# Four features computed singly at the entry of the channel mix, instead of two singly and two started early, with the block sums, splits and weight pieces there in another order

## The chip, the cores and the metric

One NeuronCore of a Trainium2 chip runs one program. The metric is the device time of one execution in microseconds; the time of a kernel is the median of its runs. Engines are named as in the profile: PE is TensorE (PEld its weight loads), ACT is ScalarE, DVE is VectorE, POOL is GpSimd, SP issues DMAs.

## What is computed

One layer of a decoder for 512 prompt rows and 64 sample rows (576 in all), width 1024: a combined projection, a short convolution, three groups of dilated attention, a gated merge, and then the part that matters here:

```python
x1 = layer_norm(ALPHA * x + mixed @ w_o, ln1_g, ln1_b)
hid = jnp.square(jax.nn.relu(x1 @ w_up))                       # 1024 -> 4096
x2 = layer_norm(ALPHA * x1 + hid @ w_down, ln2_g, ln2_b)       # 4096 -> 1024
```

## The kernel before

All matrix products are in float32 precision by splitting: an operand is held as a high half (`hi`, a cast to float32r made by ACT) and a low half (`lo` = operand minus hi, made by DVE), and a product takes three matmul passes (hi·hi, hi·lo, lo·hi). Instructions are issued in the order in which the code calls them; each engine works through its own instructions in that order and waits for semaphores. No scheduler reorders them.

Weights stand in HBM as `wall`, a list of units of 128 x 1024 floats. Units 54 to 61 are `w_o`, from `FIRST_F` = 62 on come the channel mix's: four rounds (q = 0 to 3) of eight units of `w_up` (one per feature block of 128 features) and eight of `w_down`. `Stream` loads them by SP's queue into raw tiles and splits them into `hl` tiles.

`x1` is made row tile by row tile (t = 0 to 4, the last with 64 rows): output projection, layer norm, then `turn(t)`: PE transposes the tile into the bank `x1t`, ACT and DVE write it to `yT` with gain and bias, ACT casts the high half and DVE subtracts the low half into `x1hl`. `turn(4)` comes only when the last rows are done, so the products that need just the first 256 columns of `x1hl` are put ahead of it and around it.

A feature block can be computed in two ways. *Singly* (`first_half`, `second_half`): 24 matmuls over the 256 columns `FB[0]`, 24 over the other 320, then `up_post` (ACT: relu, square, cast; DVE: low half) into `hid`. Or *as a pair* of two blocks by seven products in the place of eight (Winograd's form of Strassen's scheme, `up_pair`): the activations are split in 2 x 2 blocks (rows of the contraction by 288 columns), and four block sums of them (`x_sum(m)`: `xs` by DVE, `x1T` hi by ACT and lo by DVE) meet weight pieces `hu` (the unit itself), `hs`, `hc` (sums of weight blocks), `hd` (half a unit). The weight sums come about in `raws`: two plain DMAs by SP, then an accumulating DMA by POOL, then two additions by DVE. Products go to PSUM banks `a`, `Y`, `X`; DVE combines them in `cc`, and a second product may go into `Y` only when DVE has read the first.

`Stream.queue` takes a list of items (pairs, then units of `w_down`) and lays out weight pieces: `load()` issues what the rings of buffers allow, `hi()` casts the next piece on ACT, `lo()` does the next job on DVE (a low half or an addition). The calls to these among the products set the order on ACT and DVE.

In the kernel before, `ALONE` = 2 features (62, 63) are computed singly, and `EARLY` = (2, 4): of pairs (64, 65) and (66, 67) the two product groups `a` (24 matmuls: the first feature, the first 288 columns) are computed ahead by `up_early`, from units 64 and 66 that are loaded and split with the singles. Three pairs stand in round 0. The sequence between is written out by hand (lines 1317 to 1347).

## Time and profile before

| | |
|---|---|
| median of 3 runs | 877.98 us (877.21 to 878.64) |
| the profiled execution | 878.82 us, span 876.7 us |
| granted clock of TensorE, mean | 0.98 |
| busy: PE, DVE, ACT, POOL | 837.8, 458.3, 319.0, 79.9 us |
| HBM | 128 GB/s over the span |

The span is what the profiler saw from the first to the last instruction; the 2.12 us between it and the time of the execution lie around it. Times in the profile count from the start of the span. Below, a row of a timeline gives the start, the time from its first start to its last end, engine, line, operation, tiles, count, and in brackets the idle time before and what ended it.

### The profile page before, as it was taken

The numbers are of one execution on the slowest core, as the hardware profiler recorded it, in microseconds if no ns is written. First come the engines' busy times: TensorE is split into PE (matmuls) and PEld (weight loads), VectorE is DVE, ScalarE is ACT, GpSimd is POOL, SyncE is SP. The second block draws the span as 40 slices with busy tenths as digits, with TensorE's granted clock in tenths as the row PEclk, the third lists the DMA queues.
The fourth block names the chain that finished last, engine by engine and source line by source line (L and its number), as shares of the span: only waits on it lengthen the run. The fifth ranks groups of instructions, "written<-read, shape, count | busy, mean of one in ns | idle before, by whom it ended". The sixth has DMA issues, their size and how long they took to land.

```text
span 876.7 us, 14968 instructions
## 1 busy us (share of the span) xinstructions
PE 837.8 (96%) x6300; PEld 807.8 (92%) x6300; DVE 458.3 (52%) x755; ACT 319.0 (36%) x531; POOL 79.9 (9%) x118
## 2 busy tenths in 40 slices
PE   7999999999999999999986599999999999999994
PEld 7989989999899999988875599999999999999994
DVE  6455455465324333345655663467444754466566
ACT  6111128721222222232564461156322651256331
POOL 0221000064000000010010001000100000000013
PEclk9999999999999999999997699999999999999998
DMA  9686654851112222326061446342724254353102
GB/s 351 219 303 204 210 202 138 319 195 45 43 67 90 81 81 81 96 73 227 1 168 32 124 144 146 84 133 73 214 76 118 74 193 96 86 155 100 71 32 78
DMA packets 38610, 114.51 MB, mean 131 GB/s; under 512 B 4720, under 2 KB 5040, under 8 KB 38384
## 3 DMA queue, kind: packets, MB, share of 16 engines
q1 hardware_dynamic: 34416, 103.61, 35.8%
q0 software_dynamic: 4128, 9.96, 5.9%
q8 instruction: 49, 0.80, 0.4%
q14 instruction: 17, 0.14, 0.0%
HBM read 95.69 MB, written 16.42 MB: 128 GB/s over the span
## 4 chain that ended last, share of the span: by engine, by line
PE 90%; DVE 5%; ACT 3%; issue 1%; DMA 0%; POOL 0%; DVEq 0%; ACTq 0%
PE d L1128 18%; PE zg L518 12%; PE Y L1158 8%; PE d L1121 6%; PE a L1158 6%; PE o L1034 6%; PE X L1158 5%; PE v L885 5%; PE zA L518 5%; PE zm L518 4%; PE zB L518 4%; PE zh L518 3%; PE zc L518 2%; PE zb L518 2%; PE ya L726 1%
## 5 line engine op out<-in xcount | busy, mean ns | idle before, releaser
L1128 PE MATMUL d<-hid,hu 128*128 128x288 f32 x1152 | 154.1, 296 | 0.0
L1128 PEld LDWEIGHTS d<-hid,hu 128*128 128x128 f32 x1152 | 153.8, 189 | 0.0
L269 DVE TENSOR_TENSOR hl<-raw,hl 128x1024 fp32r<-128x1024 f32 (+1 forms) x64 | 76.3, 1203 | 102.3 <-ACT hl L268 102.0
L518 PE MATMUL zg<-xhl,hl 128*128 128x288 f32 x768 | 103.7, 296 | 0.0
L518 PEld LDWEIGHTS zg<-xhl,hl 128*128 128x128 f32 x768 | 102.8, 189 | 0.0
L268 ACT CAST hl<-raw 128x1024 fp32r<-128x1024 f32 (+1 forms) x64 | 65.0, 1020 | 67.3 <-PE zA L518 28.1
L355 ACT CAST hu<-raw 128x1024 fp32r<-128x1024 f32 x45 | 46.5, 1049 | 53.1 <-PE d L1128 27.0
L378 DVE TENSOR_TENSOR hu<-raw,hu 128x1024 fp32r<-128x1024 f32 x45 | 54.3, 1217 | 1.2 <-ACT hu L355 1.2
L1121 PE MATMUL d<-hid,hu 128*128 128x320 f32 (+1 forms) x384 | 53.4, 298 | 0.0
L1121 PEld LDWEIGHTS d<-hid,hu 128*128 128x128 f32 x384 | 51.5, 189 | 0.0
L518 PE MATMUL zA<-xhl,hl 128*128 128x288 f32 x288 | 42.8, 303 | 4.6 <-ACT xhl L496 4.5
L1158 PE MATMUL a<-x1hl,hu 128*128 128x288 f32 x312 | 46.4, 297 | 0.0
L1034 PE MATMUL o<-hl,mxhl 128*128 128x512 f32 x192 | 45.6, 394 | 0.8 <-DVE m L979 0.8
L330 POOL DMA_DIRECT2D raws<-in_wall x15 | 18.1, 1207 | 306.6 <-DMA raws<-in_wall 139.0
L518 PEld LDWEIGHTS zA<-xhl,hl 128*128 128x128 f32 x288 | 40.1, 193 | 5.7 <-ACT xhl L496 4.5
L1034 PEld LDWEIGHTS o<-hl,mxhl 128*128 128x128 f32 x192 | 35.8, 188 | 9.0 <-DVE m L979 1.1
L1158 PEld LDWEIGHTS a<-x1hl,hu 128*128 128x128 f32 x312 | 43.3, 188 | 0.4
L1376 DVE TENSOR_TENSOR yT<-yT,d 128x288 f32<-128x288 f32 x32 | 13.1, 451 | 51.7 <-PE d L1128 51.7
L1158 PE MATMUL Y<-x1T,hs 128*128 128x288 f32 x180 | 28.0, 307 | 11.0 <-DVE cc L1205 11.0
L885 PE MATMUL v<-hl,xhl 128*128 128x256 f32 x288 | 37.7, 287 | 0.0
L885 PEld LDWEIGHTS v<-hl,xhl 128*128 128x128 f32 x288 | 35.3, 191 | 2.1 <-issue 1.6
L1158 PEld LDWEIGHTS Y<-x1T,hs 128*128 128x128 f32 x180 | 26.0, 197 | 11.5 <-issue 10.7
(209 smaller groups left out, 1327.5 us busy)
## 6 DMA issues: line engine op xcount, KB each, us to landing
raw<-in_wall SPq DMA_DIRECT2D x103, 512.0 KB, 4.7
raws<-in_wall SPq DMA_DIRECT2D x30, 256.0 KB, 3.8
raws<-in_wall POOLq DMA_DIRECT2D x15, 512.0 KB, 8.4
kc<-in_kc SPq DMA_DIRECT2D x8, 512.0 KB, 4.2
out_kc_out<-kc SPq DMA_DIRECT2D x8, 512.0 KB, 6.2
vc<-in_vc SPq DMA_DIRECT2D x8, 512.0 KB, 5.4
out_vc_out<-vc SPq DMA_DIRECT2D x8, 512.0 KB, 8.2
rawl<-in_wall SPq DMA_DIRECT2D x15, 256.0 KB, 3.9
```

The lines of the kernel that those rows point to most:

```text
L268: self.nc.scalar.copy(hl[:, 0, :w], raw[:, :w])
L269: self.nc.vector.tensor_tensor(hl[:, 1, :w], raw[:, :w], hl[:, 0, :w].bitcast(F32), ALU.subtract)
L330: self.nc.gpsimd.dma_start(sums, two[:, :512].unsqueeze(1).broadcast_to((128, 2, 512)), accum_op=ALU.add)
L355: self.nc.scalar.copy(t[:, 0, :w], src[:, :w])
L378: V.tensor_tensor(t[:, 1, :w], src[:, :w], t[:, 0, :w].bitcast(F32), ALU.subtract)
L518: T.matmul(z[blk], lhsT=w[:, ws, w0 + 128 * k:w0 + 128 * k + 128], rhs=x[:, xs, k, NB * blk:NB * blk + NB], start=(k == 0 and n == 0), sto ...
L885: T.matmul(out, lhsT=rows_of(xhl, xlast, xs, k, t), rhs=wk[:, ws, kk:kk + 256], start=(k == 0 and n == 0), stop=(k == 7 and n == len(passe ...
L1034: T.matmul(out, lhsT=rows_of(mxhl, mlast, xs, k, t), rhs=w[:, ws, 512 * i:512 * i + 512], start=(k == 0 and m == 0), stop=(k == 7 and m == ...
L1121: T.matmul(z, lhsT=w[:, ws, 128 * k:128 * k + 128], rhs=x[:, xs, k, FB[blk]], start=(k == 0 and n == 0), stop=(k == 7 and n == 2), skip_gr ...
L1128: T.matmul(z[blk], lhsT=w[:, ws, 128 * k:128 * k + 128], rhs=x[:, xs, k, NB * blk:NB * blk + NB], start=(k == 0 and n == 0), stop=(k == 7 ...
L1158: T.matmul(z, lhsT=w[:, ws, w0 + 128 * i:w0 + 128 * i + 128], rhs=x(xs, i), start=(start and i == 0 and n == 0), stop=(i == 3 and n == 2), ...
L1376: V.tensor_tensor(y, y, z[blk], ALU.add)
```

## The change

It sets `ALONE` to 4 and drops `EARLY` with `up_early` and its branches: features 62 to 65 are computed singly, and two pairs are left in round 0. `turn` and `up_post` give back the low half as a step to be called later. The first pair's weight pieces are cast in the order `hs`, `hu`, `hd`, `hc` (before: `hs`, `hc`, `hd`, `hu`). The sequence at the entry is new. The diff, with what is only removed branches left out:

```diff
-ALONE = 2
-EARLY = (2, 4)
+ALONE = 4
...
-            at = v if v < FIRST_F + ALONE else FIRST_F + EARLY[v - FIRST_F - ALONE]
-            self.nc.sync.dma_start(t[:, :w], self.wall[at - 2][:, :w])
+            self.nc.sync.dma_start(t[:, :w], self.wall[v - 2][:, :w])
...
-                self.pieces += [(n, 1, "hls"), (n, 2, "hls"), (n, 3, "hl1"), (n, 0, "hls")][:3 if n < self.early else 4]
+                kinds = [(n, 1, "hls"), (n, 2, "hls"), (n, 3, "hl1"), (n, 0, "hls")]
+                self.pieces += kinds if n else [kinds[i] for i in (0, 3, 2, 1)]
...
-        for h in range(2):
-            V.tensor_tensor(lo[h], x[h], hi[h].bitcast(F32), ALU.subtract)
+
+        def low():
+            for h in range(2):
+                V.tensor_tensor(lo[h], x[h], hi[h].bitcast(F32), ALU.subtract)
+
+        return low
...
-        split_into(hid[:, 0, f, c], hid[:, 1, f, c], h)
+        S.copy(hid[:, 0, f, c], h)
+        return lambda: V.tensor_tensor(hid[:, 1, f, c], h, hid[:, 0, f, c].bitcast(F32), ALU.subtract)
...
-    def first_half(f, between=()):
+    def first_half(f):
         z = b_tile(f"u0{f}")[:, :256]
-        block(single[f], x1hl, z, 0, between)
-        up_post(f, 0, z)
+        block(single[f], x1hl, z, 0)
+        return lambda: up_post(f, 0, z)
...
-        return lambda: up_post(f, 1, z)
+        return up_post(f, 1, z)
 
-    first_half(0)
+    low = first_half(0)()
     stream.load()
-    first_half(1)
-    turn(4)
+    post = first_half(1)
+    turned = turn(4)
     rp_stack.close()
     xt_stack, xtpool = pool("xt")
     x1T = xtpool.tile([128, 2, 4, 4, NB], F32R, tag="x1T", name="x1T")
-    up_early(EARLY[0])
-    x_sum(0)
-    split = x_sum(2)
-    split[0]()
-    up_early(EARLY[1])
-    split[1]()
-    stream.hi()
-    stream.lo()
-    post = second_half(0)
+    low()
+    split[0] = x_sum(0)
+    turned()
+    split[2] = x_sum(2)
+    post()()
+    first_half(2)()()
+    split[0][0]()
+    split[0][1]()
+    first_half(3)()()
+    split[2][0]()
+    split[1] = x_sum(1)
+    split[2][1]()
+    stream.pump()
+    low = second_half(0)
     stream.lo()
     stream.lo()
-    post()
+    low()
     stream.hi()
-    S.copy(x1T[:, 0, 0], xs[0])
-    V.tensor_tensor(x1T[:, 1, 0], xs[0], x1T[:, 0, 0].bitcast(F32), ALU.subtract)
+    split[1][0]()
     stream.lo()
-    post = second_half(1)
-    split = x_sum(1)
-    split[0]()
-    post()
-    split[1]()
-    split = x_sum(3)
-    split[0]()
-    stream.hi()
-    split[1]()
-    stream.lo()
+    split[1][1]()
+    split[3] = x_sum(3)
+    low = second_half(1)
+    low()
+    stream.pump(2)
+    split[3][0]()
+    split[3][1]()
+    for f in range(2, ALONE):
+        second_half(f)()
+        stream.pump()
```

On PE, from the second single feature's first half on, there stood before the following (`u01` is the bank of feature 1's first half, `u10` of feature 0's second half, `a02` and `a04` of the early halves, `x1t40` and `x1t41` the turn of the last rows, `Y02` and `X02` of pair 64):

```order
L1121 MATMUL u01_4591<-x1hl_4110,hl63_4246 128x256 x24
L1056 MATMUL x1t40_4621<-con_63,R_4114 128x64 x4
L1056 MATMUL x1t41_4626<-con_63,R_4114 128x64 x4
L1158 MATMUL a02_4648<-x1hl_4110,hl64_4290 128x288 x24
L1158 MATMUL a04_4685<-x1hl_4110,hl65_4293 128x288 x24
L1121 MATMUL u10_4721<-x1hl_4110,hl62_4213 128x320 x24
L1121 MATMUL u11_4758<-x1hl_4110,hl63_4246 128x320 x24
L1158 MATMUL Y02_4810<-x1T_4647,hc0_4753 128x288 x12
L1158 MATMUL Y02_4810<-x1T_4647,hs0_4718 128x288 x12
L1158 MATMUL X02_4811<-x1T_4647,hs0_4718 128x288 x12
```

And now (`u02`, `u03` and `u12`, `u13` are the two more single features, 64 and 65; `a04`, `Y04` belong to pair 66):

```order
L1119 MATMUL u01_4594<-x1hl_4110,hl63_4246 128x256 x24
L1050 MATMUL x1t40_4619<-con_63,R_4114 128x64 x4
L1050 MATMUL x1t41_4624<-con_63,R_4114 128x64 x4
L1119 MATMUL u02_4656<-x1hl_4110,hl64_4290 128x256 x24
L1119 MATMUL u03_4688<-x1hl_4110,hl65_4293 128x256 x24
L1119 MATMUL u10_4725<-x1hl_4110,hl62_4213 128x320 x24
L1119 MATMUL u11_4765<-x1hl_4110,hl63_4246 128x320 x24
L1119 MATMUL u12_4803<-x1hl_4110,hl64_4290 128x320 x24
L1119 MATMUL u13_4836<-x1hl_4110,hl65_4293 128x320 x24
L1157 MATMUL a04_4867<-x1hl_4110,hu0_4757 128x288 x12
L1157 MATMUL Y04_4868<-x1T_4643,hc0_4798 128x288 x12
L1157 MATMUL a04_4867<-x1hl_4110,hu0_4757 128x288 x12
```

The two early halves gave way to two first halves, two second halves came in behind the others, and pair 64 with its five groups is gone from here.

On DVE, behind the low halves of the last rows of `x1`, there stood before the following (`xs` are block sums, `x1T` their low halves, `h02` and `h04` the early halves' activations):

```order
L549 TENSOR_TENSOR hid_4544<-h02_4675,hid_4544 128x288
L1144 TENSOR_TENSOR xs0_4680<-yT_4105 128x1152
L1148 SCALAR_TENSOR_TENSOR xs2_4682<-yT_4105,xs0_4680 128x1152
L549 TENSOR_TENSOR hid_4544<-h04_4712,hid_4544 128x288
L1153 TENSOR_TENSOR x1T_4647<-xs2_4682,x1T_4647 128x1152
L378 TENSOR_TENSOR hs0_4718<-raws64_4575,hs0_4718 128x1024
L370 TENSOR_TENSOR raws64_4575<-raws64_4575,raw64_4579 128x512
L372 TENSOR_TENSOR raws64_4575<-raws64_4575,raw64_4579 128x512
L549 TENSOR_TENSOR hid_4544<-h_01_4748,hid_4544 128x320
L1338 TENSOR_TENSOR x1T_4647<-xs0_4680,x1T_4647 128x1152
L378 TENSOR_TENSOR hc0_4753<-raws64_4575,hc0_4753 128x1024
L1146 TENSOR_TENSOR xs1_4783<-yT_4105 128x1152
```

And now, from the turn of the last rows on:

```order
L1057 TENSOR_SCALAR yT_4105<-x1t41_4624,con_63 128x64 x4
L1136 TENSOR_TENSOR hid_4544<-h_00_4570,hid_4544 128x256
L1143 TENSOR_TENSOR xs0_4645<-yT_4105 128x1152
L1068 TENSOR_TENSOR x1hl_4110<-yT_4105,x1hl_4110 128x4x64 x2
L1147 SCALAR_TENSOR_TENSOR xs2_4649<-yT_4105,xs0_4645 128x1152
L1136 TENSOR_TENSOR hid_4544<-h_10_4651,hid_4544 128x256
L1136 TENSOR_TENSOR hid_4544<-h_20_4681,hid_4544 128x256
L1152 TENSOR_TENSOR x1T_4643<-xs0_4645,x1T_4643 128x1152
L1136 TENSOR_TENSOR hid_4544<-h_30_4713,hid_4544 128x256
L1145 TENSOR_TENSOR xs1_4719<-yT_4105 128x1152
L1152 TENSOR_TENSOR x1T_4643<-xs2_4649,x1T_4643 128x1152
L372 TENSOR_TENSOR hs0_4722<-raws66_4574,hs0_4722 128x1024
```

All four block sums but the last stand now ahead of the first weight piece, the low half of the last rows of `x1` comes between two of them, and the low halves of the features fall between the sums.

On SP's queue, from the second pair's loads on, there stood before (`raws` are the weight sums, `raw` whole units, `rawl` half units; the number is the unit):

```order
L328 DMA raws66_4583<-in_wall 128x512
L329 DMA raws66_4583<-in_wall 128x512
L332 DMA raw66_4587<-in_wall 128x1024
L336 DMA rawl66_4589<-in_wall 128x512
L328 DMA raws68_4798<-in_wall 128x512
L329 DMA raws68_4798<-in_wall 128x512
L332 DMA raw68_4802<-in_wall 128x1024
L336 DMA rawl68_4804<-in_wall 128x512
L332 DMA raw70_4806<-in_wall 128x1024
L332 DMA raw71_4808<-in_wall 128x1024
```

And now:

```order
L325 DMA raws68_4582<-in_wall 128x512
L326 DMA raws68_4582<-in_wall 128x512
L329 DMA raw68_4586<-in_wall 128x1024
L333 DMA rawl68_4588<-in_wall 128x512
L329 DMA raw70_4590<-in_wall 128x1024
L329 DMA raw71_4592<-in_wall 128x1024
L329 DMA raw72_4761<-in_wall 128x1024
```

The third pair's four loads are gone, and the units of `w_down` (70 on) follow the second pair directly. POOL's queue has one accumulating DMA fewer.

## The prediction

> **What bounds the kernel now.** I read the page's first two parts, then TensorE's timeline at the entry to the channel mix, its granted clock there, and then what ACT, DVE and the queues do in the same time.

> ```profile
> span 876.7 us, 14968 instructions
> PE 837.8 (96%) x6300; PEld 807.8 (92%) x6300; DVE 458.3 (52%) x755; ACT 319.0 (36%) x531; POOL 79.9 (9%) x118
> ...
> PE   7999999999999999999986599999999999999994
> ...
> PEclk9999999999999999999997699999999999999998
> ```

> TensorE is busy 96% of the span, so only work taken from it or the slices where it isn't at 9 can move the time. In part 2 one dip lies inside the program, the 21st to 23rd slice (438 to 504 us), and in the last two of these the granted clock drops too. That is the entry to the channel mix. Its timeline on TensorE (start, duration, count, in brackets the idle time before and what ended it):

> ```profile
> 444.49 5.85 PE L1121 MATMUL u<-x1hl,hl 128*128 128x256 f32 x48
> 451.19 1.86 PE L1158 MATMUL a<-x1hl,hl 128*128 128x288 f32 x12
> 455.63 4.98 PE L1158 MATMUL a<-x1hl,hl 128*128 128x288 f32 x24 [2.57 <-ACT p L1173]
> 464.91 3.25 PE L1158 MATMUL a<-x1hl,hl 128*128 128x288 f32 x12 [4.30 <-ACT p L1173]
> 478.62 2.00 PE L1158 MATMUL Y<-x1T,hc 128*128 128x288 f32 x10 [2.55 <-DVE hc L378]
> 490.96 3.22 PE L1158 MATMUL Y<-x1T,hs 128*128 128x288 f32 x12 [10.34 <-DVE cc L1205]
> ...
> 502.37 1.87 PE L1158 MATMUL Y<-x1T,hs 128*128 128x288 f32 x12 [0.65 <-DVE cc L1205]
> 504.07 1.76 PE L1158 MATMUL X<-x1T,hs 128*128 128x288 f32 x12
> 505.67 1.76 PE L1158 MATMUL Y<-x1hl,hc 128*128 128x288 f32 x12
> ...
> 520.16 50.03 PE L1128 MATMUL d<-hid,hu 128*128 128x288 f32 x374
> ```

> The tail of one group overlaps the next, so the pace is read from starts: 504.07 to 505.67 is 1.60 us for 12 matmuls 288 wide, 0.133 us each. The first 48 matmuls 256 wide run 5.85 us with 0.16 of such tail: 0.1185 each. Per 32 columns that is some 0.0135 more, so a 320-wide one is put at 0.147 (an estimate from these two). The waits in brackets from 451.19 on add up to 2.57 + 4.30 + 2.55 + 10.34 + 0.65 = 20.41 us. After each of the four long ones a group is slow: 455.63 starts 24 matmuls that take 4.98 us where 3.20 were due, 490.96 takes 3.22 for a group of 1.60. The clock in those stretches (duration, busy and count, granted clock, DMA share, GB/s):

> ```profile
> 455.60:458.80 3.20, 3.17 (x13) 0.52 1.04 170
> 478.60:480.70 2.10, 2.00 (x10) 0.74 0.52 132
> 490.90:494.20 3.30, 3.24 (x13) 0.50 0.95 376
> ```

> So a wait of 2.5 us or more leaves the next one or two groups at half clock. From 451.19, where both kernels are still the same, to the first down-projection matmul at 520.16 are 68.97 us. The matmuls in it at full pace: 48 of 288 for the early halves (6.40), 48 of 320 (7.06), two pairs of five groups (16.00), one of seven (11.20): 40.66 us. The other 28.3 are 20.4 of waiting and 7.9 of slow clock and hand-over.

> **What the change does to TensorE's work.** Features 64 and 65 leave the scheme of seven products: 7 x 12 = 84 matmuls become 2 x 48 = 96, so 12 more, 1.60 us. In the order on TensorE from 451.19 stand now two blocks of 24 at 256 (5.69 to 5.76, I take 5.76), four of 24 at 320 (14.11; with the former 19.87) and two whole pairs of seven groups (22.40): 42.27 us if nothing waits. Without waits the down projection starts at 451.19 + 42.27 = 493.46. All rests on whether ACT, DVE and the weights keep up, so I walk them by their rows.

> ACT's rows (the relu, square and hi-cast of one block, the turn of the last rows, a cast of a block sum, a weight cast):

> ```profile
> 450.92 0.37 ACT L1135 ACTIVATE h<-u 128x256 f32<-128x256 f32 x1
> ...
> 452.08 0.38 ACT L1135 ACTIVATE h<-u 128x256 f32<-128x256 f32 x1
> ...
> 453.25 1.28 ACT L1065 ACTIVATE yT<-x1t,con 128x64 f32<-128x64 f32 x4
> 454.57 0.41 ACT L1068 CAST x1hl<-yT 128x256 fp32r<-128x256 f32 x1
> ...
> 463.41 1.15 ACT L1152 CAST x1T<-xs 128x1152 fp32r<-128x1152 f32 x1 [3.19 <-DVE xs L1148]
> ...
> 469.46 1.06 ACT L355 CAST hs<-raws 128x1024 fp32r<-128x1024 f32 x1
> 472.32 0.44 ACT L1135 ACTIVATE h<-u 128x320 f32<-128x320 f32 x1 [1.81 <-PE u L1121]
> ...
> 473.29 0.46 ACT L548 CAST hid<-h 128x320 fp32r<-128x320 f32 x1
> ...
> 486.50 0.61 ACT L355 CAST hd<-rawl 128x512 fp32r<-128x512 f32 x1
> ```

> Counting from start to start, a 256-wide feature half costs ACT 1.16 (450.92 to 452.08), a 320-wide one 1.32 (0.47 + 0.50 + 0.35, a next independent one starting 0.1 before the shown end), the turned rows 1.32 + 0.62, a block-sum cast 1.06, a weight piece 0.96, a half-size one 0.52 (0.61 in its row). In the new order ACT does from 450.92 up to the copy of the first product of pair 66: four halves of each kind (9.92), the turn (1.94), four block sums (4.24), four weight pieces (3.84), one half piece (0.52): 20.46, that is 471.4 if never idle. It waits once, for DVE's fourth block sum (468.4 by DVE's count below, against 466.9), 1.6 us with the hand-over: 473.1. TensorE finishes that product at 451.19 + 19.87 + 1.60 = 472.7, so the copy is done at about 473.6.

> DVE's rows (low halves, block sums, the addition of weight halves):

> ```profile
> 451.04 0.69 DVE L1072 TENSOR_TENSOR x1hl<-yT,x1hl 128x512 fp32r<-128x512 f32 x1 [1.22 <-ACT x1hl L1070]
> ...
> 453.72 1.09 DVE L1063 TENSOR_SCALAR yT<-x1t,con 128x64 f32<-128x64 f32 x4
> ...
> 460.63 1.35 DVE L1144 TENSOR_TENSOR xs<-yT 128x1152 f32<-128x1152 f32 x1
> 469.96 1.35 DVE L1153 TENSOR_TENSOR x1T<-xs,x1T 128x1152 fp32r<-128x1152 f32 x1
> 471.23 1.22 DVE L378 TENSOR_TENSOR hs<-raws,hs 128x1024 fp32r<-128x1024 f32 x1
> 472.48 0.69 DVE L370 TENSOR_TENSOR raws<-raws,raw 128x512 f32<-128x512 f32 x1
> 473.21 0.69 DVE L372 TENSOR_TENSOR raws<-raws,raw 128x512 f32<-128x512 f32 x1
> 473.82 0.49 DVE L549 TENSOR_TENSOR hid<-h,hid 128x320 fp32r<-128x320 f32 x1
> ...
> 487.90 0.68 DVE L378 TENSOR_TENSOR hd<-rawl,hd 128x512 fp32r<-128x512 f32 x1
> ```

> DVE takes, start to start, 1.06 for the turned rows, 0.34 and 0.41 for low halves of 256 and 320, 0.68 for the last x1 rows, 1.27 for each block sum and each of their low halves, 1.25 and 1.14 for a weight piece's low half with and without a dependent next one, 0.60 for a half piece, 0.73 + 0.61 for the two weight additions. Its new order from 451.73 (end of the 451.04 row) to the first addition from Y of pair 66: 1.06 + 4 x 0.34 + 0.68 + 8 x 1.27 + 4 x 0.41 + 2 x 1.25 + 2 x 1.14 + 0.60 + 2 x 1.34 = 22.96 us, plus 0.3 waiting for ACT's turned rows and 0.2 elsewhere: 475.2. This is the tightest place. TensorE may overwrite Y only after that addition, and by its own work gets there at 451.19 + 19.87 + 3 x 1.60 = 475.9. DVE's addition ends at 475.65, 0.2 us ahead: no wait, but nearly.

> The other meeting points of the walk: the low half of the last x1 rows is out at 455.4 and the second halves start at 456.95; the weight pieces of pair 66 are out at 465.9 (hu), 462.9 (hs), 470.6 (hc) and 469.5 (hd) against a first use at 471.1, 475.9, 472.7 and 480.8; the sums x1T at 458.9, 461.8, 467.2 and 471.9 against 475.9, 472.7, 477.5, 480.8. Pair 68: the low half of hu is out at 482.6 when TensorE asks at 482.3, a wait of 0.25. Handing over costs a few hundredths at two more places. Sum: 493.46 + 0.35 = 493.81, against 520.16: **26.35 us off**.

> The smaller edits I cost at nothing. The low halves of the turn and of each feature half go to DVE later than before, after a block sum: what hides that is the 5.76 us of the blocks of features 64 and 65; without it each block sum ahead would show with 1.27. The first pair's pieces are cast in the order hs, hu, hd, hc: in the old order hu would come last, at about 470 with TensorE asking at 471.1, so 0 to 1 us. The two pairs' squares, hi casts and low halves are 1152 instead of 864 wide, a third longer (0.25 to 0.3 each), beside groups of 1.60 that don't wait for them.

> Where instructions moved: the third pair's load, which stood behind a buffer of the first, is gone from SP's and POOL's queues (four DMAs and the accumulating one); the units behind it (70, 71) now come up directly after the second pair, so SP issues 1.05 MB more at about 449 us. That is the one cost that no row shows. It runs beside the two accumulating loads of weights:

> ```profile
> 448.67 1.27 POOL L330 DMA_DIRECT2D raws<-in_wall  x1
> 453.94 1.20 POOL L330 DMA_DIRECT2D raws<-in_wall  x1 [3.99 <-DMA raws<-in_wall]
> DMA to landing us min/median/max: 2.5/5.8/9.1
> 450.00:460.00 10.00, 7.22 (x44) 6.72 (x44) 3.31 (x9) 6.48 (x18) 1.20 (x1) 0.83 0.93 215
> 460.00:470.00 10.00, 5.70 (x27) 5.47 (x26) 3.50 (x5) 3.41 (x7) 0.00 (x0) 0.66 0.00 0
> ```

> The first such load is issued at 448.67 and lands at the latest 9.1 us on, 457.8. ACT comes to its cast at 459.6, and by the walk it may come at 460.9 before TensorE feels it. The added 1.05 MB delays it by 0 at best, and by 2.8 at worst, if all of it goes ahead at the 376 GB/s of the 490.90 row above (an estimate): 460.6. I take 0, since both ends give it. The second (453.94, so 463 to 466) is wanted at 470.9: free. Behind 493.8 the stage of the down projection is as before: a unit each 6.4 us against 0.96 + 1.14 of casting, the first unit's piece out at 484.2; cover enough, so I cost the later order at nothing.

> [...]

> **The sum.** The profiled execution took 878.82 us, 2.12 over its span; it is 0.84 over the median 877.98. 878.82 - 26.35 = 852.5 for such an execution, 851.6 against the median. I say 851.7.

> **Rivals.**
> *Late weights.* The accumulated sums of pair 66 land after 460.9. Then ACT, DVE and TensorE shift one for one: landing at 464 puts the down projection at 496.9, at 466 at 498.9, plus 1.6 of half clock once the wait passes 2.5 us. For it: the DMA share of 0.93 in the 450 to 460 row. Against: the bound above. Time 854 to 858.5.
> *Hand-overs do not add up.* The order is tight between DVE and TensorE from 471 to 483; if each of some six meetings costs 0.3 to 0.6 us more, that is 2 to 4 us, and DVE with 23.0 us of work in 24.1 has no reserve. Time 853.5 to 856. For it: before, the two lost 0.65 at 502.37. Against: the groups from 504.07 on run at their 1.60 with a pair's whole traffic beside them.
> *The change doesn't reach the entry's bound.* If what holds TensorE were the arrival of weights, the waits would only move: 876 to 879. Against: from 460 to 470 us, in the midst of the waits, DMA moves nothing (the last row above), and the waits end with DVE and ACT.
> *Slower.* The place: the whole entry on half clock. 42.27 us at half pace are 84.5, 15.6 more than the 68.97 now: 893.5. It decides once over 26.7 of the 42.27 us of work run at half clock. Against: after 455.63 one group of 12 was enough for the clock to return.

> **How the numbers follow.** Forecast 0.77 (its own range 850.8 to 853.5), late weights 0.11, hand-overs 0.09, no gain 0.015, slower 0.015. About 1.75 us (0.2%) is what can be told from no change here. Low end: no wait at all (0.35 less) and half a us of spread between runs give 850.7. High end: the first two rivals up to 856.0, which leaves out less than one in ten. Faster: 0.97; same: 0.015; slower: 0.015.

> **What the profile after would show.** Right: TensorE's first down-projection matmul near 493.8 us, no wait over 1 us between 451 and 494, the granted clock 1.00 in every 10 us window there, the first accumulating load landed by 460. Late weights: ACT idle before the cast of hs with a DMA as releaser. Hand-overs: waits of TensorE for DVE's cc or a low half. The prediction is wrong if the stage of the down projection shows waits that it does not have now, or if the clock falls though no wait reaches 2.5 us.

## The result

The changed kernel takes 852.88 us in the median of 4 runs (852.38 to 853.52), the one before 878.31 us (877.21 to 878.9): a ratio of 0.9712, 95% interval 0.9695 to 0.9729. The forecast was 851.7 us, with a range of 850.7 to 856.0.

The first parts of the page after, to set beside those of before:

```profile
span 850.7 us, 14971 instructions
PE 832.0 (98%) x6312; PEld 803.2 (94%) x6312; DVE 452.8 (53%) x747; ACT 317.0 (37%) x531; POOL 78.9 (9%) x117
...
PE   7999999999999999999999999999999999999994
...
PEclk9999999999999999999999999999999999999997
```

The dip in the middle is gone from both rows: on TensorE no slice but the first and the last is under 9, in its granted clock only the last. TensorE has 12 matmuls more (6312 for 6300) and is busy 5.8 us less, because none of those at the entry runs at half clock any more (granted clock 1.00 from 450 to 490 us, in the rows below). Its timeline at the entry:

```profile
451.62 19.95 PE L1119 MATMUL u<-x1hl,hl 128*128 128x256 f32 x144
471.40 1.76 PE L1157 MATMUL a<-x1hl,hu 128*128 128x288 f32 x12
...
476.22 1.77 PE L1157 MATMUL Y<-x1T,hs 128*128 128x288 f32 x12
...
482.64 1.83 PE L1157 MATMUL a<-x1hl,hu 128*128 128x288 f32 x12
...
493.92 21.36 PE L1126 MATMUL d<-hid,hu 128*128 128x288 f32 x159
```

From the end of the turn to the first down-projection matmul there is no bracket, so no wait is long enough to be listed. The 14 groups of the two pairs take 22.52 us (471.40 to 493.92) where 1.60 for each makes 22.40; small waits are some 0.1 us in all. The stage lasts 493.92 - 451.62 = 42.30 us, against 68.97 before. The granted clock by stretches of 10 us (duration; busy time and count of PE, PEld, DVE, ACT, POOL; clock; DMA share; GB/s):

```profile
450.00:460.00 10.00, 9.79 (x82) 9.52 (x81) 8.27 (x16) 9.71 (x22) 1.58 (x2) 1.00 1.07 315
460.00:470.00 10.00, 10.00 (x70) 10.00 (x70) 9.93 (x12) 8.36 (x14) 0.00 (x0) 1.00 0.32 84
470.00:480.00 10.00, 10.00 (x76) 10.00 (x75) 7.83 (x11) 7.03 (x14) 0.00 (x0) 1.00 0.00 0
480.00:490.00 10.00, 10.00 (x76) 9.96 (x76) 6.37 (x10) 6.73 (x9) 0.00 (x0) 1.00 0.37 107
```

The clock is 1.00 throughout, where it was 0.83, 0.66, 0.98 and 0.50. What replaced the idle time is seen in the DVE and ACT columns: DVE is busy 9.93 of 10 us from 460 to 470, where it was 3.50. From the turned rows to the end of its first addition from Y, DVE takes 23.8 us (452.08 to 475.91) where it took 37.1 (453.72 to 490.81), and TensorE has its own blocks to run meanwhile.

### The profile page after: what moved, and what is told of

Read it like the earlier page. It is cut to its first block, busy times and chain, and to the rows that moved or that the text cites. A ratio compares the mean times of both kernels' runs of the same rounds, so it can differ in the third digit from the quotient of the medians.

```text
span 850.7 us, 14971 instructions
## 1 busy us (share of the span) xinstructions
PE 832.0 (98%) x6312; PEld 803.2 (94%) x6312; DVE 452.8 (53%) x747; ACT 317.0 (37%) x531; POOL 78.9 (9%) x117
## 4 chain that ended last, share of the span: by engine, by line
PE 94%; DVE 4%; ACT 1%; DMA 0%; issue 0%; POOL 0%; ACTq 0%
PE d L1126 18%; PE zg L512 12%; PE Y L1157 8%; PE d L1119 6%; PE o L1028 6%; PE a L1157 5%; PE X L1157 5%; PE v L879 5%; PE zA L512 5%; PE zm L512 5%; PE zB L512 4%; PE zh L512 3%; PE zc L512 2%; PE zb L512 2%; PE u L1119 2%; PE ya L720 1%
## 5 line engine op out<-in xcount | busy, mean ns | idle before, releaser
L372 DVE TENSOR_TENSOR hu<-raw,hu 128x1024 fp32r<-128x1024 f32 x46 | 55.5, 1217 | 1.2 <-ACT hu L352 1.2
L1157 PE MATMUL a<-x1hl,hu 128*128 128x288 f32 x336 | 49.9, 297 | 0.0
L1157 PEld LDWEIGHTS a<-x1hl,hu 128*128 128x128 f32 x336 | 46.6, 188 | 0.3
L964 ACT ACTIVATE sg<-zg,con 128x576 f32<-128x576 f32 x16 | 11.9, 741 | 59.2 <-PE zg L512 59.2
L512 PE MATMUL zB<-xhl,hl 128*128 128x288 f32 x240 | 33.5, 297 | 0.0
```

Of the source, the lines that this page charges most:

```text
L372: V.tensor_tensor(t[:, 1, :w], src[:, :w], t[:, 0, :w].bitcast(F32), ALU.subtract)
L512: T.matmul(z[blk], lhsT=w[:, ws, w0 + 128 * k:w0 + 128 * k + 128], rhs=x[:, xs, k, NB * blk:NB * blk + NB], start=(k == 0 and n == 0), sto ...
L1157: T.matmul(z, lhsT=w[:, ws, w0 + 128 * i:w0 + 128 * i + 128], rhs=x(xs, i), start=(start and i == 0 and n == 0), stop=(i == 3 and n == 2), ...
```

## The experiments

The stage from the end of the turn (first matmul after it) to the first down-projection matmul is what each is read by; it leaves out what lies ahead, by which these runs begin the stage anywhere from 451.19 to 452.39 us. Each stage is that of one profiled execution, each median that of four runs. The kernel before, run again beside the experiments, took 877.95 to 878.88 us in the median.

| kernel | median, us | stage, us | against the changed kernel's stage |
|---|---|---|---|
| before | 878.31 | 68.97 | +26.67 |
| changed | 852.88 | 42.30 | |
| four singles, old order | 866.45 | 56.01 | +13.71 |
| two singles, new order | 868.03 | 58.55 | +16.25 |
| old order of the first pair's pieces | 853.36 | 42.94 | +0.64 |
| low halves at once | 853.03 | 42.42 | +0.12 |
| DVE later by 1, 2, 3 subtractions | 853.80, 856.48, 858.84 | 43.28, 46.19, 47.59 | +0.98, +3.89, +5.29 |
| weight sums later, three fills | 853.52 | 42.55 | +0.25 |
| weight sums later, six fills | 862.07 | 51.45 | +9.15 |

### Four singles in the old order

```diff
-    low = first_half(0)()
+    first_half(0)()()
     stream.load()
-    post = first_half(1)
-    turned = turn(4)
+    first_half(1)()()
+    turn(4)()
...
+    first_half(2)()()
+    x_sum(0)
+    split = x_sum(2)
+    split[0]()
+    first_half(3)()()
+    split[1]()
...
```

(then as before the change, with the second halves of features 64 and 65 behind it, and the first pair's weight pieces in the old order).

> Four features singly as in the changed kernel, but the steps at the entry in the order of the kernel before (low halves at once, both first block sums after the blocks, the cast of x1T of sum 0 late, weight pieces hs, hc, hd, hu). Same matmuls, same work on ACT and DVE. Theory (cover and order are both needed): walking the rows, the piece hu comes last and its low half is out about 11 us after TensorE asks for it; one group and a half then runs at half clock (3 us). The down projection starts some 56.5 us after the turn of the last rows instead of 42.3: about 867 us (863 to 870). Rival, the matmuls alone are enough: 853 to 855. Rival, the order alone is what counts: 875 or more.

866.45 us, ratio to before 0.9862 (0.9845 to 0.9879). TensorE's timeline:

```profile
482.83 0.85 PE L1156 MATMUL a<-x1hl,hu 128*128 128x288 f32 x2 [10.65 <-ACT hu L351]
484.08 2.77 PE L1156 MATMUL a<-x1hl,hu 128*128 128x288 f32 x10 [0.41 <-DVE hu L371]
486.65 2.47 PE L1156 MATMUL Y<-x1T,hc 128*128 128x288 f32 x12
```

The same matmuls, and one wait of 10.65 + 0.41 us, for the piece `hu` that ACT and DVE come to last, with half clock behind it (2.77 for ten matmuls, then 2.47, at a granted clock of 0.50 up to 488.22). The stage is 56.01 us where 56.5 was expected. The theory holds: the cover alone brings about half. Why `hu` is so late stands in ACT's rows:

```profile
473.26 1.15 ACT L1150 CAST x1T<-xs 128x1152 fp32r<-128x1152 f32 x1 [3.83 <-DVE xs L1144]
...
481.73 1.04 ACT L351 CAST hu<-raw 128x1024 fp32r<-128x1024 f32 x1
```

ACT waits 3.83 us here, and 3.09 more at 478.83, for DVE's block sums, which stand ahead of `hu` in its order; in the changed kernel it casts `hu` at 462.38. What the place of the sums and the order of the pieces are each worth beside four singles was not tried one by one.

### Two singles in the new order

```diff
 (before.py, with turn and up_post giving back the low half)
+    low()
+    split[0] = x_sum(0)
+    turned()
+    split[2] = x_sum(2)
+    post()()
     up_early(EARLY[0])
+    split[0][0]()
+    split[0][1]()
     up_early(EARLY[1])
+    split[2][0]()
+    split[1] = x_sum(1)
+    split[2][1]()
...
```

> Two features singly and the two early halves as before, three pairs, but ACT and DVE in the changed kernel's order (block sums ahead, low halves later). Theory: there are some 10 us fewer of matmuls to put between the turn and the first pair, so TensorE waits for the copies of the early products (about 2.8 and 1.1 us), for hc (2) and for DVE's first addition from Y (5 to 6), with half clock after the long ones; the down projection starts about 57 us after the turn: 867 us (863 to 871). Rival, order alone is enough: 851 to 854 (12 matmuls fewer). Rival, order alone does nothing without the singles: 875 to 878.

868.03 us, ratio 0.9886 (0.9868 to 0.9904).

```profile
456.82 4.98 PE L1163 MATMUL a<-x1hl,hl 128*128 128x288 f32 x24 [2.58 <-ACT p L1178]
462.29 1.87 PE L1163 MATMUL a<-x1hl,hl 128*128 128x288 f32 x12 [0.49 <-ACT p L1178]
...
472.30 0.53 PE L1163 MATMUL Y<-x1T,hc 128*128 128x288 f32 x2 [1.10 <-ACT hc L355]
473.55 1.60 PE L1163 MATMUL Y<-x1T,hc 128*128 128x288 f32 x10 [0.73 <-DVE hc L378]
480.89 3.25 PE L1163 MATMUL Y<-x1T,hs 128*128 128x288 f32 x12 [5.74 <-DVE cc L1210]
...
493.14 1.88 PE L1163 MATMUL Y<-x1T,hs 128*128 128x288 f32 x12 [2.08 <-DVE cc L1210]
```

The four waits that were expected are there: 2.58 and 0.49 for ACT's copies of the early products, 1.10 + 0.73 for `hc`, 5.74 for DVE's first addition from Y; a further 2.08 stands at the second pair's. The stage is 58.55 where 57 was expected: that last wait was not in the walk, the second copy was overstated. So the order alone saves 10.4 us of the stage, the cover alone 13.0, and both together 26.7, 3.3 more than the sum.

### The smaller parts: piece order and low halves

```diff
-                kinds = [(n, 1, "hls"), (n, 2, "hls"), (n, 3, "hl1"), (n, 0, "hls")]
-                self.pieces += kinds if n else [kinds[i] for i in (0, 3, 2, 1)]
+                self.pieces += [(n, 1, "hls"), (n, 2, "hls"), (n, 3, "hl1"), (n, 0, "hls")]
```

> The changed kernel with the first pair's weight pieces cast as hs, hc, hd, hu. Theory: ACT then waits for the weight additions before hc; DVE's first addition from Y comes 0.7 us later and hu's low half 0.1 us after TensorE asks: 0.3 to 0.6 us longer, 853.2 to 853.5, inside the noise of runs, and a wait of TensorE of that size in the trace. Rival (hu last is harmful, as in the other order): 3 us or more.

853.36 us, 0.5 over the changed kernel, inside the spread of runs; the trace is finer:

```profile
471.14 2.06 PE L1156 MATMUL a<-x1hl,hu 128*128 128x288 f32 x12
473.04 1.76 PE L1156 MATMUL Y<-x1T,hc 128*128 128x288 f32 x12
474.64 1.79 PE L1156 MATMUL a<-x1hl,hu 128*128 128x288 f32 x12
476.51 1.87 PE L1156 MATMUL Y<-x1T,hs 128*128 128x288 f32 x12
```

The first product runs from 471.14 to 473.04, 0.30 longer than 1.60 (its weight loads wait once, 0.3 us, for DVE's low half of `hu`, which ends at 471.55), and the fourth starts 0.27 late, for DVE's addition. The stage is 0.64 longer, of which these two show 0.57.

```diff
-    low = first_half(0)()
+    first_half(0)()()
...
-    turned = turn(4)
+    turn(4)()
...
-    low()
     split[0] = x_sum(0)
-    turned()
```

> The changed kernel with the low halves of the first feature's first half and of the last rows of x1 issued at once, ahead of the turn's rows and the first block sum, as before. Theory: DVE waits 0.5 us for ACT's cast and gets everything after it 0.7 us later; of that 0.3 us is in hand at the first addition from Y, so TensorE waits 0.4 to 0.7 there: 853.3 to 853.6. Rival, DVE has more in hand than the rows show: no wait, 852.9. Rival, the delay is passed on at each meeting: 2 us or more.

853.03 us, ratio 0.9713 (0.9698 to 0.9728). The group that needs DVE's addition starts at 477.02, 1.66 us after the one before it (475.36), so 0.06 was waited; the stage is 0.12 longer. The expectation was too high. DVE's first block sum does come 1.1 us later after the turn, but 0.7 of that is the low half of the last `x1` rows, which in the changed kernel follows the sum: the same work either way. At the addition from Y 0.3 of the delay is left, as much as DVE has in hand. This part of the change brings nothing that can be told.

### How much DVE has in hand, and what a wait costs

```diff
+    for i in range(1):      # 2 and 3 in the other two
+        V.tensor_tensor(hid[:, 0, 6:8].rearrange("p f n -> p (f n)"), yT[:, 0:2].rearrange("p f n -> p (f n)"),
+                        yT[:, 2:4].rearrange("p f n -> p (f n)"), ALU.subtract)
```

> The changed kernel with one more 128x1152 subtraction on DVE (1.27 us, its result is written where it is overwritten later) just before the first addition from Y. Theory: DVE has 0.3 us in hand there, so TensorE waits about 1.0 us once, at full clock after it: 853.9. Rival, DVE has 2 us or more in hand: 852.9.

> Two such subtractions, 2.54 us. TensorE waits about 2.2 us. By the rows of the kernel before, waits of 2.55 us were followed by clock loss; whether one of 2.2 is, is open: 855.1 without, up to 856.7 with a group at half clock. [...]

> Three such subtractions, 3.81 us. TensorE waits about 3.5 us and then runs a group at half clock: 3.5 + 1.6, 858.0. Without clock loss 856.4.

In this order TensorE's rows with one, two and three subtractions:

```profile
477.05 1.85 PE L1157 MATMUL Y<-x1T,hs 128*128 128x288 f32 x12 [0.69 <-DVE cc L1183]
```

```profile
478.19 2.24 PE L1157 MATMUL Y<-x1T,hs 128*128 128x288 f32 x12 [2.14 <-DVE cc L1183]
480.22 2.93 PE L1157 MATMUL X<-x1T,hs 128*128 128x288 f32 x12
483.00 1.77 PE L1157 MATMUL Y<-x1hl,hc 128*128 128x288 f32 x12
```

```profile
480.19 3.11 PE L1157 MATMUL Y<-x1T,hs 128*128 128x288 f32 x12 [3.49 <-DVE cc L1183]
...
485.00 1.76 PE L1157 MATMUL Y<-x1hl,hc 128*128 128x288 f32 x12
```

One subtraction (1.27) makes the stage 0.98 longer: DVE has 0.29 us in hand. The changed kernel's own row of DVE's addition from Y says the same:

```profile
475.46 0.45 DVE L1183 TENSOR_TENSOR cc<-Y,p 128x288 f32<-128x288 f32 x1
```

It ends at 475.91, and TensorE starts the group that needs it at 476.22. With two, the wait is 2.14 us in the bracket, but the stage grows by 3.89: the next two groups take 478.19 to 483.00, 4.81 us, where 3.20 are due. With three, the wait is 3.49 and the two groups take 480.19 to 485.00, again 4.81. So the loss is 1.61 us in both, for a wait of 2.14 and one of 3.49; a wait of 0.69 has none. Of the two values given for two subtractions the one with a group at half clock (856.7) is the one that came (856.48). Three were expected to add 5.1 us and added 5.29 to the stage; their median, 858.84, is 0.8 over what was expected. With two subtractions the granted clock, in stretches of 3.41 us, the time for which it stays at half, laid so that it changes at their edges (duration, busy and count of PE, clock, DMA share, GB/s):

```profile
476.01:479.43 3.42, 1.28 (x10) 1.00 0.00 0
479.43:482.84 3.41, 3.41 (x16) 0.50 0.00 0
482.84:486.25 3.41, 3.41 (x27) 1.00 0.02 5
```

The clock is still full when the matmuls come back at 478.19, falls at 479.43 and stays at half for one such stretch, 3.41 us, to 482.84. The last section takes this up.

### Weight sums that land late

```diff
+    for i in range(3):      # 6 in the second
+        G.memset(hid[:, 0, 4:8].bitcast(F32), 0.0)
     stream.load()
```

> The changed kernel with three fills of 128x2304 on POOL (into a place that is overwritten later) ahead of the first accumulating load, so that the weight sums land later by the fills' time (5 to 7 us, an estimate; the trace gives it). Theory: ACT comes to the cast of hs 0 to 1 us after the sums land now, and the walk leaves 1.2 us more before TensorE feels it; past that one for one, first at the addition from Y, later at hc. With 6 us: 3 to 4.5 us longer, 856 to 858.5 with clock loss if one wait passes 2.5 us. Rival, the sums have many us in hand: 852.9.

853.52 us, ratio 0.9708 (0.9694 to 0.9723). POOL's rows, and ACT's cast of `hs`:

```profile
449.47 6.19 POOL L1295 MEMSET hid<- 128x2304 f32 x3
455.61 2.51 POOL L327 DMA_DIRECT2D raws<-in_wall  x2
```

```profile
461.97 1.05 ACT L352 CAST hs<-raws 128x1024 fp32r<-128x1024 f32 x1 [1.29 <-DMA raws<-in_wall]
```

The fills took 6.19 us and the load was issued 6 us later than in the changed kernel, but the cast came only 1.3 us late: the sums landed 6.3 us after their issue. In the changed kernel the two accumulating loads, issued beside SP's, took (median, KB each, us to landing):

```profile
raws<-in_wall POOLq DMA_DIRECT2D x2, 512.0 KB, 9.7
```

The first of the two took 10.2, the second 9.2. So the first load, issued 6 us later, gave back some 4 of them by landing sooner. The DMA share beside it was 0.94 from 450 to 460 us and 0.52 from 460 to 470 (1.07 and 0.32 in the changed kernel); whether fewer other transfers are the reason was not tried. Of the 2 us that remain, 0.8 were in hand: in the changed kernel the sums land at 459.3 (449.11 + 10.2), and the cast comes at 460.08. The expectation did not reckon with that; 0.25 came of it in the stage. Whether late sums pass on at all was therefore tried with six fills.

> Six fills instead of three, 12.4 us by the fills' measured 2.06 each. The first accumulating load is issued some 12.3 us later than in the changed kernel and lands 5 to 6.5 us after its issue, as with three fills. Theory: ACT waits about 7.5 us before the cast of hs; 1.1 us of that is in hand, the rest is passed on to TensorE one for one (6.4), in more than one wait, of which one or two pass 2.2 us and cost 1.6 each: 861 to 862.5. Rival, the sums have several us in hand: 856 or less.

862.07 us, ratio 0.9811 (0.9793 to 0.9829). ACT's cast, and TensorE:

```profile
468.19 1.05 ACT L352 CAST hs<-raws 128x1024 fp32r<-128x1024 f32 x1 [8.11 <-DMA raws<-in_wall]
```

```profile
473.55 1.60 PE L1157 MATMUL a<-x1hl,hu 128*128 128x288 f32 x10 [1.44 <-DVE hu L372]
...
478.23 1.60 PE L1157 MATMUL Y<-x1T,hc 128*128 128x288 f32 x10 [2.27 <-DVE hc L372]
481.18 3.25 PE L1157 MATMUL a<-x1hl,hu 128*128 128x288 f32 x12 [1.35 <-ACT p L1178]
...
486.89 1.76 PE L1157 MATMUL X<-x1T,hs 128*128 128x288 f32 x12
```

ACT waited 8.11 us, and the stage is 9.15 longer: TensorE waits for `hu`, for `hc` and for the copy of the first product, and from 481.18 two groups take 5.71 us instead of 3.20. The rival is real. But it takes sums that land several us after 460, and the added loads do not bring that about.

## Why the prediction was right, point by point

**TensorE's work.** The forecast had 42.27 us of matmuls and 0.35 of waits from 451.19; the stage lasted 42.30, with no wait long enough to be listed. The 256- and 320-wide blocks together were put at 19.87 and took 19.78 (451.62 to 471.40), the two pairs at 22.40 and took 22.52.

**The walk of ACT and DVE.** Set back by the 0.43 us by which this run reached the entry later, DVE's addition from Y starts at 475.03 (forecast 475.2) and TensorE asks at 475.79 (475.9): in hand 0.31 where 0.2 was forecast, 0.29 by the experiment. The wait for `hu` of pair 68, put at 0.25, is hardly there: the group from 482.64 has no bracket and takes 1.68 us (to 484.32) where 1.60 is due. Up to the copy of the first product, ACT's only long wait is the forecast one, for the fourth block sum; the cast of `hs` has none:

```profile
460.08 1.05 ACT L352 CAST hs<-raws 128x1024 fp32r<-128x1024 f32 x1
...
468.91 1.16 ACT L1151 CAST x1T<-xs 128x1152 fp32r<-128x1152 f32 x1 [1.44 <-DVE xs L1149]
```

**The added loads.** They were let delay the sums by 0 to 2.8 us, and the time by nothing. The first accumulating load took 10.2 us to land instead of 9.1, and the cast of `hs` did not wait: taken at nothing, rightly, but with little to spare. In the three runs with subtractions, whose loads are the same, it took 11.0 to 11.3 us, and the cast waited 0.21 and 0.31 us in two of them. Nor is it shown that the added loads lengthen it: in the run with two singles in the new order, which does not have them, it took 10.5.

**The smaller edits.** The piece order is worth 0.64 us in the stage, inside the 0 to 1 given. Deferring the low halves was costed at nothing and is worth 0.12; the price of 1.27 for each block sum if their cover were gone was not tried.

**The clock.** That a wait of 2.5 us or more leaves the next groups at half clock, and a shorter one doesn't, was wrong: 2.14 us cost 1.61 with two subtractions, and 2.08 cost nothing in the run with two singles in the new order. The length of a wait alone did not tell it in these runs; the last section has what the records show beside it. The error changed nothing in the forecast time, because no wait is left.

**The remaining 1.2 us.** The forecast of 851.7 came from 26.35 off the profiled execution, less 0.84 because that execution lay over the median. Span against span 26.0 came off: 0.43 lost ahead of the entry, in code that did not change, 0.32 won in the stage, 0.24 lost behind it. The larger part is the 0.84: the profiled execution after (852.76) lies on its median, so the 0.84 was not a constant of the profiled execution, most likely only the spread of runs. It is the term of the sum that was mis-sized most; with the 0.35 that came off less between the spans (26.35 forecast, 26.0 measured) it makes the 1.2.

**The rivals.** No gain and slower are excluded by the result. Late weights cost 9.15 us in the run with six fills, but the changed kernel does not come to that. Hand-overs hardly show: no meeting point has a bracket in TensorE's timeline, and the groups of the pairs lie 0.1 us in all over their pace.

## What to carry to other kernels

When TensorE idles at a stage's entry, walk the other engines' queues by start-to-start durations from the trace, and compare what they must finish with the matmuls that can stand in between: here 23.8 us of DVE's way to its first addition from Y ran behind 24.6 us of matmuls (451.62 to 476.22), and 12 extra matmuls (1.6 us) bought cover that by itself took 13.0 us off. Order without cover took 10.4 off, both together 26.7; test both before giving either the credit. And a wait of TensorE is not priced by its length alone: here one of 2.14 us, which left 1.28 us busy of a 3.41-us stretch, cost 1.61 us of half clock on top, and one of 2.08 us, which left 2.51 and 2.24 busy in two of them, cost none.

## What was not expected of the hardware

```profile
452.28:455.70 3.42, 0.85 (x7) 1.00 0.96 201
455.70:459.11 3.41, 3.41 (x14) 0.50 1.02 166
459.11:462.52 3.41, 1.50 (x11) 1.00 0.04 8
462.52:465.94 3.42, 1.03 (x4) 0.50 0.00 0
```

The run with six fills:

```profile
472.96:476.37 3.41, 2.13 (x12) 1.00 0.51 149
476.37:479.78 3.41, 1.55 (x10) 1.00 0.01 5
479.78:483.20 3.42, 2.07 (x9) 0.50 0.00 0
483.20:486.61 3.41, 3.41 (x16) 0.50 0.00 0
```

And the run with two singles in the new order:

```profile
488.55:491.96 3.41, 2.51 (x19) 1.00 0.00 0
491.96:495.38 3.42, 2.24 (x16) 1.00 0.00 0
495.38:498.79 3.41, 3.41 (x28) 1.00 0.00 0
```

In this part of the program the clock changes at such edges only, in these three runs, in those with two and three subtractions and in the one with four singles in the old order, and the clock of a stretch went with the busy time of the one before it. After 0.85, 1.28, 1.50 and 1.55 us of 3.41 busy at full clock came a stretch at half; after 2.13, and after 1.87 at 471.48 in the run with two singles, one at full clock. Between 1.55 and 1.87 these runs have none at full clock. At half clock, the stretches with 2.07 us busy (six fills, above) and 2.28 (the kernel before, from 489.83) were followed by another at half, those with 3.41 by one at full clock.

The edges stand at fixed steps in a run (459.11 and 479.59, at which the clock changes too, are 1 and 7 steps of 3.41 us behind 455.70) and at other places in another (479.43 with two subtractions, 479.78 with six fills), and nearly the same wait went with a stretch of half clock in one run and with none in another. With two subtractions the wait of 2.14 us lies in one stretch, and the matmuls had run for 1.24 us when the clock fell at the next edge, 479.43. In the run with two singles the wait of 2.08 us ahead of 493.14 lies across the edge at 491.96, leaves 2.51 and 2.24 us busy and costs no clock. With six fills the wait of 1.35 behind the fall left 2.07 us busy, and a second stretch at half followed, 483.20 to 486.61. That the busy time of the stretch before is the cause is the author's reading: no run changes it alone.
